# Layer norm rewritten in place, its scalings on ACT, and weight lows made by ACT and an adding DMA

## The chip, the cores and the metric

The kernel runs on one core of a Trainium2 chip. The metric is the device time of one execution in microseconds; smaller is better. TensorE (PE) does the matmuls, VectorE (DVE), ScalarE (ACT) and GpSimd (POOL) the element-wise work, and SyncE (SP) issues nearly all DMAs.

## The reference

A trunk of two layers over 512 tokens of width 1024, float32. Each layer is a half-step feed-forward block, a token mixer (a bidirectional Mamba-2 scan in the first layer, differential attention in the second) and another half-step feed-forward block, each closed by a layer norm:

```python
for i in range(DEPTH):
    ...
    y = swiglu(modulate(x, mods[:, 0]), ffn_w_gate[i, 0], ffn_w_up[i, 0], ffn_w_down[i, 0])
    x = layer_norm(ALPHA * x + 0.5 * gate(0) * y, ln_g[i, 0], ln_b[i, 0])
    u = modulate(x, mods[:, 1])
    ...
    x = layer_norm(ALPHA * x + gate(1) * y, ln_g[i, 1], ln_b[i, 1])
    y = swiglu(modulate(x, mods[:, 2]), ffn_w_gate[i, 1], ffn_w_up[i, 1], ffn_w_down[i, 1])
    x = layer_norm(ALPHA * x + 0.5 * gate(2) * y, ln_g[i, 2], ln_b[i, 2])
```

Here `modulate(x, m) = x * (1 + scale) + shift`, `swiglu(u) = (silu(u @ w_gate) * (u @ w_up)) @ w_down` with an inner width of 2816, and the modulation and gate vectors come from one large projection of a condition vector (adaLN, weights `ada_w`).

## The kernel before, in words

**Layout.** Activations are kept transposed: 8 tiles (`KT`) of 128 channels by 512 tokens. `res[d]` is the residual, `u[d]` the input of the next block. The six blocks are numbered n = 0 to 5: feed-forward 0, Mamba 1, feed-forward 2 and 3, attention 4, feed-forward 5. Layer norm n follows block n.

**Products in two parts.** Matmul operands are split into a high part, rounded to the PE's fp32r format, and a low part, the rest. A product is three matmuls: high by high, high by low, low by high (`mm3`, L158 to L166). For weights, `split` (L102) makes the parts: ACT copies the loaded tile `raw` into `wh` (L119), which rounds it, and DVE subtracts `wh` from `raw` into `wl` (L120). `raw` has 4 buffers in turn, `wh` and `wl` have 3, and 3 more inside a feed-forward block.

**Feed-forward block** (`ffn`, L502). The inner width is worked in three parts of 8, 7 and 7 tiles (`FPARTS`). For each part the kernel first makes the hidden tiles, then does that part's down projection: 8 units, one per output tile d, each with its own weight load (`wdn`), split and 24 or 21 matmuls of 512 columns, and a DVE instruction that adds the result to the residual (`add_res`, L366). "First phase" and "second phase" below are the down projections of the first two parts, `pi` 0 and 1; the third ends in the layer norm. The first hidden tiles of a block are plain (gate and up products, `L535`); from index `first7` on (10 in block 0, otherwise 4) each hidden tile is made with seven products instead of eight, from sums of inputs (`input_forms`, L421, made during the last four plain tiles: DVE L426 to L431, then split by ACT L149 and DVE L150) and sums of weights (`weight_forms`, L442: DVE L459, split by ACT L449 and DVE L450).

**The adaLN stream.** In blocks 0, 2 and 3 the adaLN weights are worked off between other work: `advance(stream, per[1])` puts two of them behind each unit of the first two down projections. Each is one 512 KB load through `raw` and one DVE instruction (L180). Block 5 has none.

**Layer norm** (class `LN`, L260). In the last down projection DVE, ACT and POOL gather the sums as tiles come out (`start`, `feed`); the last units are done in two halves of 256 tokens so that one half's norm runs beside the other half's matmuls. `stats` forms the reciprocal deviation `rb`, spread over the partitions in the PSUM, and centres `res`. `normalize` (L324) then makes the next block's inputs, per tile and half: DVE `t = res * G * rb` (L348), ACT `uh = t + B` (L349), DVE `ul = (t + B) - uh` (L350); ACT copies `rb` into `rs` (L353). `residual` (L355) leaves the scaled residual: two POOL instructions per tile, L359 and L360, 16 per layer norm, needed only by the next block's first `add_res`.

**Order.** Each engine works its own queue in order. The order in the queues is the scheduler's, from the order of the program text and the dependences; a wait at the head of a queue holds all behind it.

Of the kernel before, what the change touches and what calls it, by code (L numbers as in the profile page):

```python
# [46 lines left out]
def hybrid_trunk(tc, xT, cb, par, cst, adaw, wgu, wdn0, wdn1, wdn2, wdt, win, wso, wqk, wv, wao, dist_in, dtp, lam_in, out):  # L47
    nc = tc.nc
    ctx = ExitStack()
    wdn = (wdn0, wdn1, wdn2)  # L50

    cp = ctx.enter_context(tc.tile_pool(name="cp", bufs=1))
    ap = ctx.enter_context(tc.tile_pool(name="ap", bufs=NA))
# [11 lines left out]
    def tmp(name="tmp"):  # L65
        return tp.tile([P, T], F32, tag="t", name=name)
# [24 lines left out]
    def load(src, n=1024):  # L91
        raw = wp.tile([P, 1024], F32, tag="raw", name="raw", bufs=4)
        nc.sync.dma_start(raw[:, :n], src)
        return raw[:, :n]
# [6 lines left out]

    def split(raw, where=None):  # L102

        n = raw.shape[-1]
        if where == "a":
            hi, lo = [], []
            for o in range(0, n, T):
                r = raw[:, o : o + T]
                h, l = big(F32R, "wah"), big(F32R, "wal")
                x = nc.scalar.activation(h, r, AF.Copy)  # L110
                eng = nc.vector if first_split[0] or o else nc.gpsimd
                y = eng.tensor_tensor(out=l, in0=r, in1=h.bitcast(F32), op=ALU.subtract)  # L112
                for a, b in zip((x, y), behind):
                    tc.add_manual_dep(a.ins, b.ins.name, NOSYNC, reason="inputs before weights")
                hi.append(h)
                lo.append(l)
            return [(hi[c // T][:, c % T : c % T + P], lo[c // T][:, c % T : c % T + P]) for c in range(0, n, P)]
        hi, lo = ring()
        nc.scalar.activation(hi[:, :n], raw, AF.Copy)  # L119
        nc.vector.tensor_tensor(out=lo[:, :n], in0=raw, in1=hi[:, :n].bitcast(F32), op=ALU.subtract)  # L120
        return Unit(hi, lo, n)

    def ring():
# [61 lines left out]
    onep, shift, gvec, lnG, lnB, lnag, lnab = {}, {}, {}, {}, {}, {}, {}  # L185
# [74 lines left out]
    class LN:  # L260
# [63 lines left out]
        def normalize(self, a, b, rb):  # L324
            n = self.n
            if n == 5:
                for d in range(KT):
                    t = res[d][:, a:b]
                    nc.vector.scalar_tensor_tensor(
                        out=t, in0=t, scalar=pc(C_LNG + n * 8 + d), in1=rb, op0=ALU.mult, op1=ALU.mult  # L330
                    )
                    nc.scalar.activation(t, t, AF.Identity, bias=pc(C_LNB + n * 8 + d))
                    if d % 2:
                        nc.sync.dma_start(
                            out[(d - 1) * P : (d + 1) * P, a:b].rearrange("(e p) t -> p e t", e=2),
                            resid[:, d - 1 : d + 1, a:b],
                        )
                return
            if self.u is None:
                self.u = [  # L340
                    tuple(ap.tile([P, T], F32R, tag="u", name=x, bufs=2 * KT) for x in ("uh", "ul")) for _ in range(KT)
                ]
                self.rs = ap.tile([P, T], F32, tag="l", name="rs", bufs=3)
            for d in range(KT):
                G, B = lnG[n][:, d : d + 1], lnB[n][:, d : d + 1]
                t = tmp("lt")[:, a:b]
                uh, ul = self.u[d][0][:, a:b], self.u[d][1][:, a:b]
                nc.vector.scalar_tensor_tensor(out=t, in0=res[d][:, a:b], scalar=G, in1=rb, op0=ALU.mult, op1=ALU.mult)  # L348
                nc.scalar.activation(uh, t, AF.Identity, bias=B)  # L349
                nc.vector.scalar_tensor_tensor(  # L350
                    out=ul, in0=t, scalar=B, in1=uh.bitcast(F32), op0=ALU.add, op1=ALU.subtract
                )
            nc.scalar.activation(self.rs[:, a:b], rb, AF.Copy)  # L353

        def residual(self):  # L355
            n = self.n
            if n < 5:
                for d in range(KT):
                    nc.gpsimd.tensor_tensor(out=res[d], in0=res[d], in1=self.rs, op=ALU.mult)  # L359
                    nc.gpsimd.tensor_scalar(  # L360
                        out=res[d], in0=res[d], scalar1=lnag[n][:, d : d + 1],
                        scalar2=lnab[n][:, d : d + 1], op0=ALU.mult, op1=ALU.add,
                    )

    def add_res(d, pd, n, a, b):
        nc.vector.scalar_tensor_tensor(  # L366
# [135 lines left out]
    def ffn(n, stream=None, per=(0, 0), pre=None, first7=FT):  # L502


        forms, making = [], None
        sc = ExitStack()
        extra[0] = sc.enter_context(tc.tile_pool(name=f"wx{n}", bufs=3))
        idx = {0: 0, 2: 1, 3: 2, 5: 3}[n]
        u = next_u[0]
        f = 0  # L510
        pre = pre or first_units(n)
        for pi, nf in enumerate(FPARTS):
            hs = []
            open7 = None
            for _ in range(nf):
                if f >= first7:
                    g = seven(load(wgu[idx, f, 0]), load(wgu[idx, f, 1]), forms, hs)
                    next(g)
                    if open7 is not None:
                        next(open7, None)  # L520
                    next(g)
                    open7 = g
                    f += 1
                    continue
                wg, wu = (pre.pop(0) if pre else split(load(wgu[idx, f, e])) for e in range(2))
                cols = HALVES if f < 3 and n > 0 else FULL
                tag = "mid" if f == 2 else "ln" if f == 3 and n == 0 else "acc"
                pg = acc(tag)
                proj(pg, wg, u, cols=cols)
                pu = acc(tag)  # L530
                proj(pu, wu, u, cols=cols)
                sg = tmp("sg")
                nc.scalar.activation(sg, pg, AF.Silu)
                h = tmp("h")
                nc.vector.tensor_tensor(out=h, in0=sg, in1=pu, op=ALU.mult)  # L535
                hs.append(split_act(h))
                if first7 - 4 <= f < first7:
                    making = making or input_forms(u)
                    forms.append(next(making))
                f += 1  # L540
                if f > 3 or n > 0:
                    advance(stream, per[0])

            if open7 is not None:
                next(open7, None)

            def mk(d):
                return lambda: [(d, split(load(wdn[pi][idx, d], nf * P)))]

            for _ in down_units(n, hs, [mk(d) for d in range(KT)], pi == len(FPARTS) - 1):  # L550
                if pi < 2:
                    advance(stream, per[1])
        extra[0] = None
        sc.close()
# [13 lines left out]
    def ssm(n):  # L568
# [244 lines left out]
        def run(units):  # L813
            for f in units:
                f()
# [6 lines left out]
        dt_chain(pd)  # L822
        run(units_x(0, xs)[2:])
        silu(bc + xs)
        run(units_z(0, zs[0])[:2])
        cur = prepare(0, xs, bc)
        outs, yrs = {}, {}
# [48 lines left out]
    def attention(n):  # L876
# [6 lines left out]
        lt = tmp("lam")  # L883
# [21 lines left out]
        def unit_v(p_):  # L905
            def f():
                w = [split(load(wv[p_, e])) for e in range(2)]
                V[p_] = []
                for b in range(2):
                    pv = acc()  # L910
                    prev = None
                    for t2 in range(2):
                        c = slice((b * 2 + t2) * P, (b * 2 + t2 + 1) * P)
                        terms = []
                        for k in range(KT):
                            wh, wl = w[k // 4].cols((k % 4) * 256, (k % 4 + 1) * 256)
                            terms.append((u[k][0][:, c], u[k][1][:, c], wh, wl))
                        prev = mm3(pv[:, t2 * 256 : (t2 + 1) * 256], terms, prev)
                    V[p_].append(split_act(pv))
            return f  # L920
# [61 lines left out]
        for e in range(2):  # L982
            unit_qk(0, e, HALVES, pre[e])()
        unit_v(0)()
        os_ = {}
        og = []

# [174 lines left out]
```

## Time and profile before

| what | value |
|---|---|
| time, median of 3 runs | 2262.34 us (2256.63 to 2265.38) |
| profiled execution, its own time | 2255.55 us |
| its span, first to last instruction | 2253.7 us |
| PE busy | 2166.1 us (96%) |
| DVE busy | 1817.0 us (81%) |
| ACT busy | 1013.4 us (45%) |
| POOL busy | 407.7 us (18%) |
| DMA moved | 297.02 MB, mean 132 GB/s |

Busy time is the time in which an engine executes; issuing and waiting do not count. A line such as `L120 DVE TENSOR_TENSOR wl<-raw,wh ... x210 | 258.3, 1231 | 81.6` names source line, engine, operation, output and inputs, count, busy time in us, mean of one in ns, and the idle time of the engine just before, with what ended it.

### The profile page before, as it was taken

The numbers are of one execution on the slowest core, as the hardware profiler recorded it, in microseconds if no ns is written. First come the engines' busy times: TensorE is split into PE (matmuls) and PEld (weight loads), VectorE is DVE, ScalarE is ACT, GpSimd is POOL, SyncE is SP. The second block draws the span as 40 slices with busy tenths as digits, with TensorE's granted clock in tenths as the row PEclk, the third lists the DMA queues.
The fourth block names the chain that finished last, engine by engine and source line by source line (L and its number), as shares of the span: only waits on it lengthen the run. The fifth ranks groups of instructions, "written<-read, shape, count | busy, mean of one in ns | idle before, by whom it ended". The sixth has DMA issues, their size and how long they took to land.

```text
span 2253.7 us, 34668 instructions
## 1 busy us (share of the span) xinstructions
PE 2166.1 (96%) x13462; PEld 1886.2 (84%) x13462; DVE 1817.0 (81%) x2982; ACT 1013.4 (45%) x1696; POOL 407.7 (18%) x412
## 2 busy tenths in 40 slices
PE   7999999999999998999999899999999999899998
PEld 5789898866777687999999889899877779889897
DVE  6889898656765689889889998997866679959696
ACT  4324353567656534344453334344555544425353
POOL 3000004344322335000015200003300025000003
PEclk9999999999999989999999999999999999999999
DMA  8873733564544413546442273733211111223231
GB/s 301 273 271 104 242 111 110 123 174 139 168 122 123 134 47 113 196 160 201 146 131 82 79 256 99 244 101 115 67 57 57 57 66 57 103 85 106 92 114 46
DMA packets 88549, 297.02 MB, mean 132 GB/s; under 512 B 9536, under 2 KB 12992, under 8 KB 88384
## 3 DMA queue, kind: packets, MB, share of 16 engines
q1 hardware_dynamic: 88384, 294.81, 40.9%
q8 instruction: 105, 1.72, 0.3%
q14 instruction: 60, 0.49, 0.1%
HBM read 289.53 MB, written 5.24 MB: 131 GB/s over the span
## 4 chain that ended last, share of the span: by engine, by line
PE 55%; DVE 16%; issue 4%; ACT 3%; DMA 2%; POOL 2%; POOLq 0%; ACTq 0%; DVEq 0%; SPq 0%
PE acc L162 44%; PE mid L162 5%; DVE wl L120 2%; PE mid L782 2%; DVE raw L459 2%; DVE lo L150 1%; DVE wl L450 1%; DVE ul L350 1%; DMA raw<-in_wdn 1%; DVE raw L180 1%; PE mid L931 1%; PE ln L162 1%; DVE lt L348 1%; ACT wh L119 1%; PE ln L249 1%
## 5 line engine op out<-in xcount | busy, mean ns | idle before, releaser
L162 PE MATMUL acc<-hi,wh 128*128 128x256 f32 (+1 forms) x1584 | 535.8, 339 | 20.2 <-ACT wh L449 10.0
L162 PE MATMUL acc<-hi,wl 128*128 128x256 f32 (+1 forms) x1584 | 534.9, 338 | 5.6 <-DVE wl L450 5.6
L162 PE MATMUL acc<-lo,wh 128*128 128x256 f32 (+1 forms) x1584 | 533.8, 337 | 1.3 <-DVE lo L150 1.3
L162 PE MATMUL acc<-uh,wh 128*128 128x256 f32 (+1 forms) x1160 | 396.3, 342 | 6.6 <-ACT px L482 6.6
L162 PE MATMUL acc<-ul,wh 128*128 128x256 f32 (+1 forms) x1160 | 393.5, 339 | 0.2 <-DVE ul L1039 0.2
L162 PE MATMUL acc<-uh,wl 128*128 128x256 f32 (+1 forms) x1160 | 391.7, 338 | 1.4 <-DVE wl L120 1.4
L119 ACT ACTIVATE wh<-raw 128x1024 fp32r<-128x1024 f32 (+1 forms) x210 | 213.6, 1023 | 310.7 <-DMA raw<-in_wdn 122.0
L162 PEld LDWEIGHTS acc<-hi,wh 128*128 128x128 f32 x1584 | 304.2, 192 | 58.0 <-ACT wh L449 10.6
L162 PEld LDWEIGHTS acc<-hi,wl 128*128 128x128 f32 x1584 | 304.4, 192 | 36.8 <-DVE wl L450 6.3
L162 PEld LDWEIGHTS acc<-lo,wh 128*128 128x128 f32 x1584 | 304.3, 192 | 33.0 <-DVE lo L150 3.2
L120 DVE TENSOR_TENSOR wl<-raw,wh 128x1024 fp32r<-128x1024 f32 (+1 forms) x210 | 258.3, 1231 | 81.6 <-ACT wh L119 73.4
L449 ACT ACTIVATE wh<-raw 128x1024 fp32r<-128x1024 f32 x198 | 208.7, 1059 | 249.7 <-DVE raw L459 134.3
L450 DVE TENSOR_TENSOR wl<-raw,wh 128x1024 fp32r<-128x1024 f32 x198 | 240.7, 1219 | 33.5 <-ACT wh L449 32.6
L162 PEld LDWEIGHTS acc<-uh,wh 128*128 128x128 f32 x1160 | 222.0, 191 | 39.3 <-issue 9.0
L162 PEld LDWEIGHTS acc<-uh,wl 128*128 128x128 f32 x1160 | 222.1, 192 | 27.8 <-issue 3.9
L162 PEld LDWEIGHTS acc<-ul,wh 128*128 128x128 f32 x1160 | 222.4, 192 | 26.0 <-issue 4.7
L180 DVE SCALAR_TENSOR_TENSOR raw<-raw,cond 128x1024 f32<-128x1024 f32 x144 | 179.3, 1256 | 14.4 <-DMA raw<-in_adaw 13.8
L459 DVE TENSOR_TENSOR raw<-raw 128x512 f32<-128x512 f32 x264 | 183.3, 696 | 5.5
L366 DVE SCALAR_TENSOR_TENSOR resid<-acc,gv,resid 128x512 f32<-128x512 f32 (+1 forms) x172 | 113.0, 659 | 61.1 <-PE acc L162 60.6
L112 POOL TENSOR_TENSOR wal<-raw,wah 128x512 fp32r<-128x512 f32 x13 | 20.9, 1612 | 598.5 <-ACT wah L110 598.4
L277 POOL TENSOR_TENSOR resid<-resid,m 128x512 f32<-128x512 f32 x12 | 20.0, 1687 | 583.5 <-ACT m L274 581.9
L162 PE MATMUL mid<-uh,wh 128*128 128x256 f32 (+2 forms) x380 | 108.6, 286 | 1.4 <-DVE up L491 1.4
(270 smaller groups left out, 4234.8 us busy)
## 6 DMA issues: line engine op xcount, KB each, us to landing
raw<-in_wgu SPq DMA_DIRECT2D x176, 512.0 KB, 4.0
raw<-in_adaw SPq DMA_DIRECT2D x144, 512.0 KB, 4.6
raw<-in_wdn SPq DMA_DIRECT2D x64, 448.0 KB, 3.8
raw<-in_win SPq DMA_DIRECT2D x40, 512.0 KB, 4.4
raw<-in_wdn SPq DMA_DIRECT2D x32, 512.0 KB, 4.4
rw<-scr SPq DMA_DIRECT2D x32, 512.0 KB, 5.5
ch<-scr SPq DMA_DIRECT2D x32, 256.0 KB, 3.7
raw<-in_wso SPq DMA_DIRECT2D x16, 512.0 KB, 3.5
```

The lines of the kernel that those rows point to most:

```text
L119: nc.scalar.activation(hi[:, :n], raw, AF.Copy)
L120: nc.vector.tensor_tensor(out=lo[:, :n], in0=raw, in1=hi[:, :n].bitcast(F32), op=ALU.subtract)
L150: y = nc.vector.tensor_tensor(out=lo, in0=src, in1=hi.bitcast(F32), op=ALU.subtract)
L162: last = nc.tensor.matmul(o, lhsT=a, rhs=b, start=start and j == 0, stop=j == n - 1, skip_group_check=not start)
L180: nc.vector.scalar_tensor_tensor(out=raw, in0=raw, scalar=1.0, in1=cond, op0=ALU.mult, op1=ALU.mult, accum_out=mods[l][:, j : j + 1],)
L249: nc.tensor.matmul(o[:, j * P : (j + 1) * P], lhsT=cols[:, j : j + 1].broadcast_to([P, P]), rhs=ident, start=True, stop=True)
L348: nc.vector.scalar_tensor_tensor(out=t, in0=res[d][:, a:b], scalar=G, in1=rb, op0=ALU.mult, op1=ALU.mult)
L366: nc.vector.scalar_tensor_tensor(out=res[d][:, a:b], in0=pd[:, a:b], scalar=gvec[n][:, d : d + 1], in1=res[d][:, a:b], op0=ALU.mult, op1=A ...
L449: nc.scalar.activation(x[0], r, AF.Copy)
L450: nc.vector.tensor_tensor(out=x[1], in0=r, in1=x[0].bitcast(F32), op=ALU.subtract)
L459: nc.vector.tensor_tensor(out=o, in0=x, in1=y, op=ALU.add)
L782: nc.tensor.matmul(py[hh * 64 : (hh + 1) * 64, cc], lhsT=lhs, rhs=rhs, start=k == 0, stop=k == 2)
```

## The change

It does three things. First, `normalize` multiplies `res` by `rb` in place on DVE (one plain multiplication), and ACT then makes two scaled copies, `uh = G * z + B` in fp32r and `t = G * z + B` in float32; DVE subtracts, `ul = t - uh`. The copy `rs` goes. Second, since `res` now holds the normalized value, the residual is one ACT instruction per tile, `res = lnag * res + lnab`, and POOL has no part in it. These eight instructions are kept in a list `later` and put into the program text behind the next block's first units: two after each of the first four hidden tiles of a feed-forward block, all behind the first SiLUs of the Mamba block, and behind the first value unit of the attention block. Third, in the first two down projections of every feed-forward block the low part of a weight is made without DVE: ACT writes `-raw`, rounded, into `wl`, and a DMA issued by POOL adds `raw` to it in the SBUF. The scratch for DMAs issued this way grows from 1024 to 4096 bytes.

```diff
@@ split @@
         hi, lo = ring()
         nc.scalar.activation(hi[:, :n], raw, AF.Copy)
-        nc.vector.tensor_tensor(out=lo[:, :n], in0=raw, in1=hi[:, :n].bitcast(F32), op=ALU.subtract)
+        if where == "dma":
+            nc.scalar.activation(lo[:, :n], raw, AF.Copy, scale=-1.0)
+            nc.gpsimd.dma_start(lo[:, :n].bitcast(F32), raw, accum_op=ALU.add)
+        else:
+            nc.vector.tensor_tensor(out=lo[:, :n], in0=raw, in1=hi[:, :n].bitcast(F32), op=ALU.subtract)
         return Unit(hi, lo, n)
@@ LN.normalize, LN.residual @@
-                self.rs = ap.tile([P, T], F32, tag="l", name="rs", bufs=3)
             for d in range(KT):
                 G, B = lnG[n][:, d : d + 1], lnB[n][:, d : d + 1]
-                t = tmp("lt")[:, a:b]
+                z, t = res[d][:, a:b], tmp("lt")[:, a:b]
                 uh, ul = self.u[d][0][:, a:b], self.u[d][1][:, a:b]
-                nc.vector.scalar_tensor_tensor(out=t, in0=res[d][:, a:b], scalar=G, in1=rb, op0=ALU.mult, op1=ALU.mult)
-                nc.scalar.activation(uh, t, AF.Identity, bias=B)
-                nc.vector.scalar_tensor_tensor(
-                    out=ul, in0=t, scalar=B, in1=uh.bitcast(F32), op0=ALU.add, op1=ALU.subtract
+                nc.vector.tensor_tensor(out=z, in0=z, in1=rb, op=ALU.mult)
+                for o in (uh, t):
+                    nc.scalar.activation(o, z, AF.Identity, bias=B, scale=G)
+                nc.vector.tensor_tensor(out=ul, in0=t, in1=uh.bitcast(F32), op=ALU.subtract)
+
+        def residual(self):
+            n = self.n
+            def mk(d):
+                return lambda: nc.scalar.activation(
+                    res[d], res[d], AF.Identity, bias=lnab[n][:, d : d + 1], scale=lnag[n][:, d : d + 1]
                 )
-            nc.scalar.activation(self.rs[:, a:b], rb, AF.Copy)
-
-        def residual(self):
-            n = self.n
-            if n < 5:
-                for d in range(KT):
-                    nc.gpsimd.tensor_tensor(out=res[d], in0=res[d], in1=self.rs, op=ALU.mult)
-                    nc.gpsimd.tensor_scalar(
-                        out=res[d], in0=res[d], scalar1=lnag[n][:, d : d + 1],
-                        scalar2=lnab[n][:, d : d + 1], op0=ALU.mult, op1=ALU.add,
-                    )
+            later.extend(mk(d) for d in range(KT) if n < 5)
+
+    later = []
+
+    def scale_residual(k=KT):
+        for f in later[:k]:
+            f()
+        del later[:k]
@@ ffn @@
                 f += 1
+                scale_residual(2 if f < 5 else KT)
                 if f > 3 or n > 0:
                     advance(stream, per[0])
...
-                return lambda: [(d, split(load(wdn[pi][idx, d], nf * P)))]
+                return lambda: [(d, split(load(wdn[pi][idx, d], nf * P), "dma" if pi < 2 else None))]
@@ ssm @@
         silu(bc + xs)
+        scale_residual()
@@ attention @@
         unit_v(0)()
+        scale_residual()
@@ kernel @@
-    nc = bacc.Bacc("TRN2", target_bir_lowering=False, num_devices=1, dynamic_dma_scratch_size=1024)
+    nc = bacc.Bacc("TRN2", target_bir_lowering=False, num_devices=1, dynamic_dma_scratch_size=4096)
```

More of the change, by code (lines that the diff above doesn't have):

```diff
@@ L342, in normalize @@
                 ]
-                self.rs = ap.tile([P, T], F32, tag="l", name="rs", bufs=3)
             for d in range(KT):
                 G, B = lnG[n][:, d : d + 1], lnB[n][:, d : d + 1]
-                t = tmp("lt")[:, a:b]
+                z, t = res[d][:, a:b], tmp("lt")[:, a:b]
                 uh, ul = self.u[d][0][:, a:b], self.u[d][1][:, a:b]
-                nc.vector.scalar_tensor_tensor(out=t, in0=res[d][:, a:b], scalar=G, in1=rb, op0=ALU.mult, op1=ALU.mult)
-                nc.scalar.activation(uh, t, AF.Identity, bias=B)
-                nc.vector.scalar_tensor_tensor(
-                    out=ul, in0=t, scalar=B, in1=uh.bitcast(F32), op0=ALU.add, op1=ALU.subtract
-                )
-            nc.scalar.activation(self.rs[:, a:b], rb, AF.Copy)
+                nc.vector.tensor_tensor(out=z, in0=z, in1=rb, op=ALU.mult)
+                for o in (uh, t):
+                    nc.scalar.activation(o, z, AF.Identity, bias=B, scale=G)
+                nc.vector.tensor_tensor(out=ul, in0=t, in1=uh.bitcast(F32), op=ALU.subtract)
         def residual(self):
             n = self.n
-            if n < 5:
-                for d in range(KT):
-                    nc.gpsimd.tensor_tensor(out=res[d], in0=res[d], in1=self.rs, op=ALU.mult)
-                    nc.gpsimd.tensor_scalar(
-                        out=res[d], in0=res[d], scalar1=lnag[n][:, d : d + 1],
-                        scalar2=lnab[n][:, d : d + 1], op0=ALU.mult, op1=ALU.add,
-                    )
+            def mk(d):
+                return lambda: nc.scalar.activation(
+                    res[d], res[d], AF.Identity, bias=lnab[n][:, d : d + 1], scale=lnag[n][:, d : d + 1]
+                )
+            later.extend(mk(d) for d in range(KT) if n < 5)
[4 more added lines that the diff above has]
+        del later[:k]
     def add_res(d, pd, n, a, b):
```

## The prediction, made before the changed kernel was run

> **What bounds the kernel now.** I read the page first: parts 1 and 2.
>
> ```profile
> span 2253.7 us, 34668 instructions
> PE 2166.1 (96%) x13462; PEld 1886.2 (84%) x13462; DVE 1817.0 (81%) x2982; ACT 1013.4 (45%) x1696; POOL 407.7 (18%) x412
> PE   7999999999999998999999899999999999899998
> DVE  6889898656765689889889998997866679959696
> ```
>
> PE is the bound: 96% busy, so at most 2253.7 - 2166.1 = 87.6 us can be won without touching the matmuls. A change to DVE, ACT, POOL and DMA counts only where PE waits for them. So I looked at stretches where PE is idle while DVE is full. Busy time by stretch gives three, each at the start of a feed-forward block that follows a layer norm (n=1, 2 and 4); the last line is their sum:
>
> ```profile
> 860.00:900.00 40.00, 31.41 (x195) 28.28 (x194) 40.00 (x52) 14.37 (x22) 25.03 (x13) 0.89 0.35 112
> 1255.00:1275.00 20.00, 13.54 (x72) 11.90 (x71) 19.86 (x32) 9.43 (x13) 0.00 (x0) 0.87 0.22 79
> 1915.00:1936.00 21.00, 15.33 (x73) 13.05 (x72) 20.90 (x32) 8.88 (x12) 5.65 (x4) 0.83 0.14 51
> sum 81.00, PE 60.27 PEld 53.23 DVE 80.76 ACT 32.69 POOL 30.68; mean PE 20.09 PEld 17.74 DVE 26.92 ACT 10.90 POOL 10.23
> ```
>
> The columns after the length are PE, PEld, DVE, ACT, POOL, granted clock, DMA share and GB/s. PE is idle for 81.00 - 60.27 = 20.7 us while DVE is busy for 80.76 of 81. The clock column adds a second loss: 0.11 x 40 + 0.13 x 20 + 0.17 x 21 = 10.6 us. Together 31.3 us, the most that these three places can return. Why DVE is late there shows in its instructions by line. The first six rows are one such start, 1226.3 to 1253.8; the next two are whole-run means of clean 512 and 256 wide operations; then come two rows of the page and the two POOL rows of the residual:
>
> ```profile
> L350 DVE SCALAR_TENSOR_TENSOR ul<-lt,lnB,uh 128x256 fp32r<-128x256 f32 x2 | 3.0, 1516 | 0.0
> L150 DVE TENSOR_TENSOR lo<-h,hi 128x512 fp32r<-128x512 f32 x2 | 2.5, 1231 | 0.0
> L426 DVE TENSOR_TENSOR fb<-uh,ul 128x512 f32<-128x512 f32 x2 | 2.5, 1228 | 0.0
> L431 DVE TENSOR_TENSOR fb<-fb 128x256 f32<-128x256 f32 x2 | 2.3, 1167 | 0.0
> L429 DVE TENSOR_TENSOR ft<-ft,fb 128x256 f32<-128x256 f32 x2 | 2.3, 1166 | 0.0
> L180 DVE SCALAR_TENSOR_TENSOR raw<-raw,cond 128x1024 f32<-128x1024 f32 x1 | 2.3, 2303 | 0.0
> L150 DVE TENSOR_TENSOR lo<-sg,hi 128x512 fp32r<-128x512 f32 x66 | 45.3, 687 | 7.0 <-ACT hi L149 7.0
> L490 DVE TENSOR_TENSOR px<-acc,px 128x256 f32<-128x256 f32 x66 | 27.7, 420 | 0.1
> L350 DVE SCALAR_TENSOR_TENSOR ul<-lt,lnB,uh 128x256 fp32r<-128x256 f32 x80 | 45.4, 593 | 0.7 <-ACT uh L349 0.4
> L180 DVE SCALAR_TENSOR_TENSOR raw<-raw,cond 128x1024 f32<-128x1024 f32 x144 | 179.3, 1256 | 14.4 <-DMA raw<-in_adaw 13.8
> L360 POOL TENSOR_SCALAR resid<-resid,lnag,lnab 128x512 f32<-128x512 f32 x40 | 70.5, 1770 | 0.0
> L359 POOL TENSOR_TENSOR resid<-resid,rs 128x512 f32<-128x512 f32 x40 | 62.0, 1570 | 39.0 <-ACT rs L353 39.0
> ```
>
> While POOL scales the residual, DVE operations on two tiles of the SBUF take up to twice their clean time. In this one start that is 2 x (1231 - 687) + 2 x (1228 - 687) + 2 x (1167 - 420) + 2 x (1166 - 420) + (2303 - 1256) + 2 x (1516 - 593) = 8.0 us of DVE time, against the 6.5 us that PE idles there.
>
> **The residual's move.** It takes 80 POOL instructions away, 16 per layer norm, about 8 x (1.77 + 1.57) = 26.7 us each time. With them go the 8.0 us of DVE stretch per start; DVE, not POOL, was on the path. The relief is more than PE's idle in two of the starts and about as much in the first (8.6 us), and a PE that does not stop keeps its clock. I take 28 of the 31.3 us. What would be late next is ACT: the 8 scalings land on it, priced by a 512-wide ACT operation, 8 x 0.63 = 5.0 us per layer norm.
>
> ```profile
> L149 ACT ACTIVATE hi<-sg 128x512 fp32r<-128x512 f32 x66 | 41.5, 629 | 43.9 <-DVE sg L498 43.9
> L348 DVE SCALAR_TENSOR_TENSOR lt<-resid,lnG,ln 128x256 f32<-128x256 f32 x80 | 35.1, 474 | 1.6 <-PE ln L249 1.5
> L349 ACT ACTIVATE uh<-lt,lnB 128x256 fp32r<-128x256 f32 x80 | 36.9, 502 | 35.2 <-DVE lt L348 35.0
> PE acc L162 <- ACT uh L349: 2.2, 3, 1.1
> PE acc L162 <- DVE ul L350: 1.6, 2, 0.8
> ```
>
> ACT is busy 32.7 of 81 us in the three stretches, so its idle time covers the 5.0 us; uncovered, PE could wait behind one pair of scalings, 1.3 us per start. In the Mamba and attention blocks the same 5.0 us follow the first SiLUs and the first value unit: I take zero, with bounds of 5 us lost in either and 3 us won.
>
> **The in-place norm.** Per half tile DVE had 0.474 + 0.593 = 1.07 us; it gets two plain operations like the 0.420 row, 0.84. ACT had 0.502 and gets two, 1.00. So a tile leaves at ACT's 1.00 us instead of DVE's 1.07: nothing. The last two rows (whole run, waits of PE) show all that PE waits for inputs there: 2.2 + 1.6 = 3.8 us, which bounds the gain; the same amount again bounds the loss, if ACT is held up by its squares.
>
> **The lows by ACT and the adding DMA.** For 64 units DVE loses one subtraction (1.1 to 1.2 us), ACT gains one pass (0.95 to 1.06 us), POOL's queue gains one issue. What I had to settle is whether the loads keep up, so I read DMA, DVE, ACT and PE in time order around the two phases of block 2. The first row is block 0's first phase:
>
> ```profile
> 121.00:158.00 37.00, 37.00 (x162) 30.25 (x161) 30.11 (x48) 8.50 (x8) 0.00 (x0) 1.00 0.87 296
> 928.69 0.33 SPq L93 DMA_DIRECT2D raw<-in_wdn  x1
> ...
> 935.32 2.40 SPq L93 DMA_DIRECT2D raw<-in_adaw  x2
> 939.20 0.33 SPq L93 DMA_DIRECT2D raw<-in_wdn  x1
> 932.97 1.06 ACT L119 ACTIVATE wh<-raw 128x1024 fp32r<-128x1024 f32 x1 [0.91 <-DMA raw<-in_wdn]
> 934.07 1.23 DVE L120 TENSOR_TENSOR wl<-raw,wh 128x1024 fp32r<-128x1024 f32 x1 [0.71 <-ACT wh L119]
> 946.39 0.75 DVE L366 SCALAR_TENSOR_TENSOR resid<-acc,gv,resid 128x512 f32<-128x512 f32 x1
> 1043.94 0.95 ACT L119 ACTIVATE wh<-raw 128x896 fp32r<-128x896 f32 x1 [3.56 <-DMA raw<-in_wdn]
> 1060.72 0.50 PE L162 MATMUL acc<-hi,wh 128*128 128x512 f32 x1 [0.99 <-ACT hi L149]
> raw<-in_adaw SPq DMA_DIRECT2D x144, 512.0 KB, 4.6
> raw<-in_wdn SPq DMA_DIRECT2D x32, 512.0 KB, 4.4
> scr<-rows SPq DMA_DIRECT2D x2, 1024.0 KB, 9.2
> out<-resid SPq DMA_DIRECT2D x8, 256.0 KB, 2.2
> ```
>
> PE is full in that window (37.00 of 37.00, 162 matmuls, 0.228 us each), so DVE's relief buys nothing here; ACT, busy 8.50 of 37, has room for its second pass. The larger scratch for POOL's DMA issue costs no time that any row here prices. A unit is 24 matmuls, 5.48 us, in a first phase and 21, 4.80 us, in a second. In blocks 0, 2 and 3 each unit brings three loads (weights, two adaLN rows) through four buffers, in order. So a weight load's buffer is wanted again by the first adaLN load of the next unit, behind which stands the weight load after that. The rows show this: weights at 928.69, buffer free when DVE's subtraction ends (935.3), adaLN issued at 935.32, weights two units on at 939.20. Period: 10.5 / 2 = 5.25 us a unit.
>
> After the change the buffer is held until the adding DMA lands. Call x the time from the end of ACT's second pass to that landing. The period becomes (4.4 load + 2.1 for two ACT passes + x + 1.5 for the issues behind it) / 2; those issues took 3.9 us before (935.32 to 939.20) because adaLN buffers came free late, and a longer period takes that wait away, leaving issues of 0.33 us and their gaps. No row shows x. Below it is bounded by 2.2 us (256 KB out of the SBUF), above by 9.2 us (1024 KB out of the SBUF, as many bytes as the add reads). Nearest is a 512 KB load in these same stretches, 4.6 us; with 0.6 us for POOL's issue, about twice SP's 0.33, I take x = 5.2. Period: 13.2 / 2 = 6.6 us.
>
> That is slower than PE, but the weights are ahead. In block 2's first phase the second unit's ACT pass starts at 932.97 and PE has finished the first unit at 946.4 at the latest; I use 946. After: ready at 932.97 + 2.1 + 5.2 = 940.3, 5.7 us ahead. Over the six units that follow, the supply falls back 6 x (6.6 - 5.48) = 6.7 us: 1.0 us lost. In its second phase: 1043.94 + 1.9 + 5.2 = 1051.0 against 1061, 10.0 ahead; 6 x (6.6 - 4.80) = 10.8: 0.8 us lost. I let these two stand for the three blocks: 3 x 1.8 = 5.4 us. Each phase then hands on no lead, so the next gate and up weights, loaded behind the last unit, come late: an estimate of 1 us each, 6 us. Loss: 11.4 us. Block 5 has no adaLN loads; four weight buffers held for (4.4 + 2.1 + 5.2) give 11.7 / 4 = 2.9 us a unit, under 4.80: nothing. POOL has no other work in these windows (0.00), so nothing queues behind its waiting issue.
>
> **The sum**, on the profiled execution (2255.55 us): 2255.6 - 28 + 11.4 = 2239. That execution is 0.3% under the median shown, 2262.34, so I add half of that difference: 2242. The rivals' times below are on the profiled execution's scale.
>
> **Rivals.** (a) The adding DMA is slower, and the change loses. Adding means reading both tiles. These rows price 256 KB more at 3.5 - 2.5 = 1.0 us, the second read of 512 KB at 2.0 us:
>
> ```profile
> raw<-in_wso SPq DMA_DIRECT2D x16, 512.0 KB, 3.5
> raw<-in_wdt SPq DMA_DIRECT2D x1, 256.0 KB, 2.5
> ```
>
> Then x = 7.2, the period 7.6 us; the leads shrink to 3.7 and 8.0 us and the fall-back grows to 12.7 and 16.8: 9.0 + 8.8 lost per block, 53 in three, 59 with the hand-on: 2255.6 - 28 + 59 = 2287. It decides from x = 5.9 up, where loss and gain are level. For it: the DMA share is 0.87 at 296 GB/s already, so a further transfer lengthens the loads too. Against it: SBUF reads may be quicker than HBM's. The Trainium skill ("Collectives: The Full Stack", The bandwidth ceiling) says an adding transfer issues two source reads per chunk on one ring and so ran at about half a copy's rate; by it this rival holds. No transfer in this trace adds, so the trace cannot confirm it. (b) The add hides wholly: x under 4 us, period under 6.0, no loss: 2255.6 - 31 = 2225. For it: 2.2 us for a small transfer out of the SBUF. (c) Most of the 28 us does not come: the forms wait for ACT (its scalings in front of the splits) where they waited for DVE. With 10 us gained and the 11.4 lost: 2257. Against it: ACT's 60% idle there.
>
> **Chances.** My sum 0.34, (a) 0.31, (b) 0.16, (c) 0.19. A measurement of this kernel tells about 0.5% (11 us) from no change. Of my case 0.28 is faster and 0.06 the same; (b) is faster; (c) is 0.16 same, 0.03 slower; (a) is slower. Faster 0.44, same 0.22, slower 0.34. Range: from (b) with some of the norm's 3.8 us, 2222, to (a) with a little more, 2292; my own case alone 2230 to 2256.
>
> **What would show it.** Residual: no POOL work after the layer norms, the 256-wide DVE operations of the forms near 0.42 us, PE idle gone and its clock at 1.00 after 860, 1255 and 1915. Lows: the time from issue to landing of the POOL-issued DMA with its queue (my x, 5.2 us), SP waiting for that DMA in place of DVE L120, weight loads 6.6 us apart, PE still full in block 2's phases. I am wrong if x passes 5.9 us, if PE's waits for the low tile of the down projection exceed 15 us in all, or if the three starts still idle with ACT named.

## The result: 2.7% slower

| what | before | after |
|---|---|---|
| time, median of the runs side by side | 2261.61 us (2256.63 to 2265.38) | 2322.83 us (2319.84 to 2326.74) |
| ratio, 95% interval | | 1.0273 (1.0247 to 1.0299) |
| profiled execution | 2255.55 us | 2324.32 us |

61 us were lost where 20 us of gain were predicted; the time lies outside the predicted range (2222 to 2292). Of the eight executions of e4_raw5 below one was in the chip's slow state (2965.76 us at a granted clock of 0.654), so its time is the median of the other seven, 2272.21 us; with the eighth it is 2273.55, from which the 49 and the 60 us in two later expectations come. The page of the changed kernel, its first lines, the slices of PE and DVE, and its DMA queues:

```profile
span 2322.5 us, 34945 instructions
PE 2186.1 (94%) x13462; PEld 1898.5 (82%) x13462; DVE 1704.3 (73%) x2918; ACT 1135.3 (49%) x1870; POOL 329.5 (14%) x396
PE   7989989999999989988999998889999998999998
DVE  6859598656766689677688958678776678948496
q1 hardware_dynamic: 88384, 294.81, 39.6%
q0 software_dynamic: 9216, 31.46, 7.4%
```

DVE was relieved as meant (1817.0 to 1704.3 us). But PE, the bound, now stands still for 2322.5 - 2186.1 = 136 us instead of 88, and its busy time rose by 20 us for the same 13462 matmuls, at a lower granted clock behind the pauses (rows below).

**Where the time went.** I cut both spans at the first and the last matmul of each down projection phase (PE `acc<-hi,wl`, 128x512) and subtracted. Between these profiled executions the difference is 68.8 us (7.6 more than between the medians).

| stretch | after - before, us |
|---|---|
| from the last down projection ahead to the first one of blocks 2, 3 and 5 (the mixers, the layer norms, the three starts) | -24.3 |
| the first phases of blocks 0, 2 and 3 | +30.9 |
| the second phases of these blocks | +3.1 |
| the six stretches of hidden tiles behind these phases | +54.5 |
| block 5 behind its start | +4.6 |

The start gain came, most of it. The starts, by stretches of the changed kernel that cover the input forms (columns as in the prediction), and three of the forms' rows in the second of them:

```profile
890.00:930.00 40.00, 39.18 (x280) 36.55 (x278) 40.00 (x67) 24.37 (x36) 0.00 (x0) 1.00 0.38 119
1285.00:1319.00 34.00, 34.00 (x240) 31.84 (x240) 32.03 (x58) 19.34 (x29) 0.00 (x0) 1.00 0.25 81
1970.00:2003.00 33.00, 33.00 (x235) 30.97 (x234) 32.57 (x56) 21.50 (x33) 0.00 (x0) 1.00 0.21 69
```

```profile
L436 DVE TENSOR_TENSOR fb<-uh,ul 128x512 f32<-128x512 f32 x4 | 2.7, 684 | 0.0
...
L441 DVE TENSOR_TENSOR fb<-fb 128x256 f32<-128x256 f32 x4 | 1.7, 420 | 0.0
...
L439 DVE TENSOR_TENSOR ft<-ft,fb 128x256 f32<-128x256 f32 x4 | 1.7, 418 | 0.0
```

POOL is gone, the operations that took 1228 and 1167 ns take 684 and 420, and PE idles 0.8 us of 107 at full clock.

The loss is not mainly inside the phases whose weights were changed. More than half of it lies in the hidden tiles behind them. These stretches by windows, first two of before (of block 2, then the sum of all six), then the same of the changed kernel:

```profile
982.60:1051.80 69.20, 69.20 (x578) 68.88 (x578) 64.08 (x102) 32.99 (x51) 0.00 (x0) 1.00 0.40 129
1093.60:1162.80 69.20, 69.20 (x578) 68.89 (x578) 60.80 (x93) 34.43 (x53) 0.00 (x0) 1.00 0.35 108
...
sum 424.90, PE 421.12 PEld 414.32 DVE 381.92 ACT 204.17 POOL 0.00; mean PE 70.19 PEld 69.05 DVE 63.65 ACT 34.03 POOL 0.00
```

```profile
1017.40:1094.80 77.40, 71.05 (x580) 70.10 (x579) 66.55 (x108) 37.80 (x56) 2.61 (x3) 0.96 0.49 142
1136.00:1213.80 77.80, 73.29 (x578) 72.38 (x577) 70.17 (x105) 38.77 (x57) 0.00 (x0) 0.93 0.36 110
...
sum 479.30, PE 437.94 PEld 427.23 DVE 418.54 ACT 231.02 POOL 7.77; mean PE 72.99 PEld 71.21 DVE 69.76 ACT 38.50 POOL 1.29
```

The same 578 matmuls filled 69.20 us without a gap before. Now PE idles 479.3 - 437.9 = 41.4 us in the six (3.8 before), and needs 16.8 us more for the same matmuls at a clock of 0.93 to 0.96. What it waits for, from the changed kernel's waits of PE, and of ACT; then ACT's timeline from 1084 to 1096:

```profile
PE acc L167 <- DMA wl<-raw: 18.9, 8, 5.6
PE acc L167 <- ACT sg L498: 18.0, 6, 5.5
...
PE acc L167 <- ACT hi L154: 11.5, 8, 2.9
PE acc L167 <- ACT px L492: 9.9, 5, 3.7
```

```profile
ACT wh L120 <- DMA raw<-in_wdn: 184.2, 46, 10.2
```

```profile
1089.07 0.95 ACT L120 ACTIVATE wh<-raw 128x896 fp32r<-128x896 f32 x1 [8.14 <-DMA raw<-in_wdn]
1089.93 0.40 ACT L507 ACTIVATE sg<-px 128x256 f32<-128x256 f32 x1
1090.23 0.93 ACT L122 ACTIVATE wl<-raw 128x896 fp32r<-128x896 f32 x1
1091.09 0.63 ACT L154 ACTIVATE hi<-sg 128x512 fp32r<-128x512 f32 x1
1091.62 0.36 ACT L498 ACTIVATE sg<-acc 128x256 f32<-128x256 f32 x1
```

Only 18.9 us are a wait for a low. The other rows are hidden-tile work on ACT (SiLU, copies and splits). The timeline shows why it is late at the end of such a stretch: the pass of a late weight, the third of the next phase, stands at the head of ACT's queue, 8.14 us without its data, and the SiLUs behind it wait too. PE, which waits for `sg`, idles 5.5 us there (from 1086.5). Before, that weight's pass stood behind the SiLU in the queue, and waited 0.21 us:

```profile
1047.87 0.42 ACT L497 ACTIVATE sg<-px 128x256 f32<-128x256 f32 x1 [2.70 <-DVE px L496]
1048.50 0.95 ACT L119 ACTIVATE wh<-raw 128x896 fp32r<-128x896 f32 x1 [0.21 <-DMA raw<-in_wdn]
```

So it is not only the load that came later: in blocks 2 and 3 the scheduler also put the pass ahead of the SiLU. DVE's queue added to it. The instruction that makes this SiLU's input (`px`, L506) ended at 1087.4, behind an adaLN instruction that had waited 1.97 us for its load; over the whole run DVE waited 136.8 us for adaLN loads, 13.8 before. In the six stretches together PE waits 16 us for `sg`, nearly all at their ends, and 25 us for other work, most of it near their starts, where the gate and up weights come late.

The adding DMA itself, by POOL's group and the medians from issue to landing:

```profile
L123 POOL DMA_DIRECT2D wl<-raw x64 | 55.6, 869 | 891.5 <-ACT wl L122 525.4
...
raw<-in_wdn SPq DMA_DIRECT2D x32, 512.0 KB, 5.1
wl<-raw POOLq DMA_DIRECT2D x32, 512.0 KB, 7.0
...
wl<-raw POOLq DMA_DIRECT2D x32, 448.0 KB, 6.4
```

With the 0.3 us that POOL starts behind ACT, x is 7.3 us for a full unit and 6.7 for a short one, 7.0 on average. The queue q0 took 0.074 x 2322.5 x 16 = 2750 us of engine time for 64 transfers, 43 us each or 2.7 us of all 16 engines; the loads of q1 come to 1.6 us of all 16 per 512 KB.

### The profile page after: what moved, and what is told of

It is laid out like the page before. It is cut to its first block, busy times and chain, and to the rows that moved or that the text cites. A ratio compares the mean times of both kernels' runs of the same rounds, so it can differ in the third digit from the quotient of the medians.

```text
span 2322.5 us, 34945 instructions
## 1 busy us (share of the span) xinstructions
PE 2186.1 (94%) x13462; PEld 1898.5 (82%) x13462; DVE 1704.3 (73%) x2918; ACT 1135.3 (49%) x1870; POOL 329.5 (14%) x396
## 5 line engine op out<-in xcount | busy, mean ns | idle before, releaser
L167 PE MATMUL acc<-hi,wl 128*128 128x256 f32 (+1 forms) x1584 | 540.9, 342 | 24.3 <-DMA wl<-raw 18.9
L185 DVE SCALAR_TENSOR_TENSOR raw<-raw,cond 128x1024 f32<-128x1024 f32 x144 | 177.8, 1238 | 145.8 <-DMA raw<-in_adaw 136.8
L167 PEld LDWEIGHTS acc<-uh,wl 128*128 128x128 f32 x1160 | 221.8, 191 | 26.7 <-issue 3.9
L125 DVE TENSOR_TENSOR wl<-raw,wh 128x1024 fp32r<-128x1024 f32 (+1 forms) x146 | 178.7, 1224 | 51.1 <-ACT wh L120 42.7
L123 POOL DMA_DIRECT2D wl<-raw x64 | 55.6, 869 | 891.5 <-ACT wl L122 525.4
L376 DVE SCALAR_TENSOR_TENSOR resid<-acc,gv,resid 128x512 f32<-128x512 f32 (+1 forms) x172 | 112.9, 658 | 41.4 <-PE acc L167 41.0
L167 PE MATMUL mid<-uh,wl 128*128 128x256 f32 (+2 forms) x380 | 107.5, 283 | 0.0
```

What stands on the lines that cost most here:

```text
L123: nc.gpsimd.dma_start(lo[:, :n].bitcast(F32), raw, accum_op=ALU.add)
L167: last = nc.tensor.matmul(o, lhsT=a, rhs=b, start=start and j == 0, stop=j == n - 1, skip_group_check=not start)
L185: nc.vector.scalar_tensor_tensor(out=raw, in0=raw, scalar=1.0, in1=cond, op0=ALU.mult, op1=ALU.mult, accum_out=mods[l][:, j : j + 1],)
L376: nc.vector.scalar_tensor_tensor(out=res[d][:, a:b], in0=pd[:, a:b], scalar=gvec[n][:, d : d + 1], in1=res[d][:, a:b], op0=ALU.mult, op1=A ...
```

## The experiments

Twelve runs, each timed beside the kernel before on the same chip. The columns behind the ratio are microseconds against before in the profiled executions, cut as above (to about 0.2 us): the starts with the mixers ahead, the six phases, the six stretches of hidden tiles behind them. Below, "the norm part" is the in-place norm with the residual on ACT.

| kernel | us | ratio to before (95%) | starts | phases | hidden |
|---|---|---|---|---|---|
| changed kernel | 2322.83 | 1.0273 (1.0247 to 1.0299) | -24.3 | +34.0 | +54.5 |
| e1_norm: norm part alone | 2226.48 | 0.9853 (0.9837 to 0.9870) | -31.6 | +1.0 | +2.1 |
| e2_lows: lows alone | 2353.12 | 1.0416 (1.0393 to 1.0439) | +11.4 | +33.2 | +51.6 |
| e3_block5: lows in block 5 only | 2230.81 | 0.9873 (0.9853 to 0.9893) | -33.8 | +2.9 | +2.9 |
| e8_pool: residual by one POOL instruction | 2225.96 | 0.9851 (0.9836 to 0.9866) | -30.0 | +1.0 | +1.0 |
| e9_pooltwo: by two POOL instructions | 2254.18 | 0.9977 (0.9967 to 0.9986) | -4.6 | -0.2 | +1.5 |
| e10_noscale: before, no residual scaling | 2224.78 | 0.9849 (0.9834 to 0.9863) | -34.6 | +1.2 | +0.6 |
| e5_copy: copying DMA in place of the adding | 2270.12 | 1.0063 (1.0035 to 1.0092) | -33.5 | +14.3 | +33.2 |
| e4_raw5: changed, five load buffers | 2272.21 | 1.0056 (1.0036 to 1.0077) | -37.0 | +16.9 | +27.8 |
| e7_traffic: norm part + adding traffic | 2269.70 | 1.0049 (1.0033 to 1.0066) | -32.8 | +17.3 | +26.7 |
| e13_hold: norm part + buffer held | 2266.87 | 1.0031 (1.0017 to 1.0046) | -34.6 | +24.0 | +25.0 |
| e11_raw3: norm part, three load buffers | 2286.43 | 1.0115 (1.0092 to 1.0137) | -24.3 | +9.1 | +41.3 |
| e12_raw5: norm part, five load buffers | 2213.28 | 0.9797 (0.9783 to 0.9812) | -36.0 | -5.1 | -7.2 |

**The two parts.** First the norm part alone, then the lows alone:

```diff
-                return lambda: [(d, split(load(wdn[pi][idx, d], nf * P), "dma" if pi < 2 else None))]
+                return lambda: [(d, split(load(wdn[pi][idx, d], nf * P), None))]
```

> The changed kernel with its lows made by DVE again in every phase; the norm in place and the residual on ACT stay. Theory (the loss lies in the lows, the stretch of DVE beside POOL's residual was real): 28 us under before, about 2234, the three starts (feed-forward 2, 3, 5) without PE idle and with a full clock. Rival (the residual on ACT itself delays the blocks): within 10 us of before, 2252 to 2272.

> The kernel before with only the lows of the first two down projections made by ACT and the adding DMA (scratch 4096). Theory that the two parts add: the changed kernel is 61 us slower, the norm part wins 28, so this is 89 us slower than before, about 2351. Rival, that they depend on each other (PE reaches the phases earlier when the starts are shorter, so the weights' lead is spent there): under 75 us slower, below 2337.

They came to -34 us and +93 us; together 59, against the measured 61. So the parts add, the norm part beats both kernels, and the loss belongs to the lows alone. (e2_lows is the kernel before with only the other branch of `split` and the larger scratch, which e1_norm has too, without a loss.)

**Block 5**, where there is no adaLN stream:

```diff
+                ... "dma" if pi < 2 and n == 5 else None ...
```

> The changed kernel with the adding DMA in block 5 alone, where no adaLN loads run. Both theories of the loss (the DMA engines are full; the buffers are held) need those loads: within 5 us of the run with the norm alone. Rival (the add's own latency of about 7 us or ACT's second pass costs PE): 15 us or more slower than it, a quarter of the loss of 70 or more.

2230.81, 4 us above the norm part, with intervals that overlap. In the profiled executions, which lie 8.2 us apart, block 5's first phase is 5.8 us longer and the hidden tiles behind it 1.5 us. The same DMA costs little where the load stream is thin.

**Is POOL the cause of the idle starts?** The gain could also come from cheaper DVE instructions in the norm. First the norm part with the residual by one POOL instruction per tile:

```diff
-            later.extend(mk(d) for d in range(KT) if n < 5)
+            for d in range(KT if n < 5 else 0):
+                nc.gpsimd.tensor_scalar(
+                    out=res[d], in0=res[d], scalar1=lnag[n][:, d : d + 1],
+                    scalar2=lnab[n][:, d : d + 1], op0=ALU.mult, op1=ALU.add,
                 )
```

> As the run with the norm alone, but POOL scales the residual, one TENSOR_SCALAR per tile at the old place instead of two instructions (about 14 of 26.7 us of POOL per layer norm). Theory (DVE is stretched while POOL works): half of the gain is lost, 2244 to 2252, the stretched DVE operations are there for half as long. Rival (the gain comes from DVE's cheaper instructions in the norm): the same time as the run with the norm alone, within 5 us.

The whole gain stayed, though POOL still worked 62.8 us:

```profile
L362 POOL TENSOR_SCALAR resid<-resid,lnag,lnab 128x512 f32<-128x512 f32 x40 | 62.8, 1586 | 18.8 <-ACT lt L354 18.8
```

By that alone the prediction's cause could have been wrong, for POOL still worked beside DVE: at block 3's start from 1216.6 to 1230.3, and the forms began at 1227.1. (The next expectation calls POOL done before the forms start; this trace shows 3.2 us of overlap.) So two more kernels: the norm part with two POOL instructions per tile again (first times a tile of ones), and the kernel before with the residual's scaling left out, a part that it then does not compute.

> The in-place norm as in the change, the lows by DVE, and the residual back on POOL with two instructions per tile (times a tile of ones, then scale and bias), so that POOL works about as long as before, 26 us per layer norm. Theory 'POOL beside DVE': with POOL's long work back beside the forms, the gain of 34 us shrinks to 5 to 10 us, near 2250 to 2256, and the starts of blocks 2, 3 and 5 go back up by 6 to 10 us each. Theory 'cheaper norm on DVE' (the gain comes from tensor_tensor in place of scalar_tensor_tensor): it stays near 2227. One POOL instruction per tile kept the whole gain, with POOL done before the forms start; if two keep it too, POOL is not the cause.

> The kernel before with the residual's scaling left out (that part isn't computed), norm and lows as before. Theory 'POOL beside DVE': the gain of the starts comes with this alone, 28 us or more off, near 2230. Theory 'cheaper norm on DVE': near before, 2255 to 2260. If both contribute, between, 2235 to 2250.

With two instructions 28 of the 34 us were back (2254.18). Without any residual work, and with the old norm, the gain was whole (2224.78; -35.5 against -34.0, intervals overlapping). POOL's work on the residual is the cause; the norm's instructions are at most a small part (e9_pooltwo, which has the new ones, is 5 us under before). The starts of e9_pooltwo by windows, then some rows of DVE and POOL in one of them, in order of time:

```profile
866.00:902.00 36.00, 31.89 (x213) 29.11 (x211) 35.93 (x55) 15.49 (x24) 10.62 (x7) 0.96 0.29 97
1237.00:1275.00 38.00, 34.72 (x230) 31.98 (x230) 37.90 (x60) 14.65 (x23) 13.71 (x8) 0.96 0.22 71
1898.00:1935.00 37.00, 33.27 (x222) 31.03 (x221) 36.83 (x54) 15.05 (x24) 13.74 (x8) 0.94 0.21 71
```

```profile
1242.90 1.87 POOL L366 TENSOR_SCALAR resid<-resid,lnag,lnab 128x512 f32<-128x512 f32 x1
1243.08 1.21 DVE L463 TENSOR_TENSOR wl<-raw,wh 128x1024 fp32r<-128x1024 f32 x1
...
1244.74 1.45 POOL L365 TENSOR_TENSOR resid<-resid,onez 128x512 f32<-128x512 f32 x1
...
1244.96 1.77 DVE L158 TENSOR_TENSOR lo<-ft,hi 128x512 fp32r<-128x512 f32 x1
1246.66 0.41 DVE L444 TENSOR_TENSOR fb<-fb 128x256 f32<-128x256 f32 x1
```

DVE's subtraction of 1244.96, 0.68 us when clean, began 0.22 us after POOL's multiplication of two tiles and ended 0.54 us after that one's end (1246.19): it did most of its work behind it. Beside POOL's other instruction, the scale and bias of one tile, the subtraction of 1243.08 took 1.21 us, its clean time. It is so over the whole run. In e9_pooltwo 58 DVE operations on two SBUF tiles overlapped the multiplication and took 75.8 us together, 39.2 when clean; 44 met only the scale and bias and took 31.0 us, 30.4 when clean; in e8_pool 73 met it and took 56.0 us, 48.7 when clean. So the stretch comes nearly all from the instruction on two tiles, and this, more than an earlier end, is why one instruction per tile cost nothing. No run has two instructions on one tile each to test it alone.

The Trainium skill ("SBUF — State Buffer", SBUF: two separate sides) says that DVE operations with two SBUF inputs and GpSimd share ports under an exclusive lock, held for a whole instruction. The rows beside the multiplication agree; those beside the scale and bias, which reads the SBUF too, do not (1.21 us begun 0.18 us after it).

**Two reads?** The add replaced by a copy (the low part is then the whole weight):

```diff
-            nc.gpsimd.dma_start(lo[:, :n].bitcast(F32), raw, accum_op=ALU.add)
+            nc.gpsimd.dma_start(lo[:, :n].bitcast(F32), raw)
```

> The changed kernel with a plain copying DMA in place of the adding one: same issue, same 512 KB written, but the low part is then the whole weight, not the rest. If the add pays for two reads: engine time per DMA falls from 43 to about 26 us (that of a load of the same size), landing from issue from 7.0 to about 5.3 us, the time to about 2280. If the cost is POOL's issue and the queue, not the second read: landing stays above 6.3 us and the time above 2305.

```profile
q0 software_dynamic: 7168, 31.46, 3.6%
...
wl<-raw POOLq DMA_DIRECT2D x32, 512.0 KB, 5.5
...
wl<-raw POOLq DMA_DIRECT2D x32, 448.0 KB, 5.1
```

The copy takes half the engine time (3.6 against 7.4%) and lands 1.5 us sooner; the Trainium skill's rule of two source reads ("Collectives: The Full Stack", The bandwidth ceiling), which the prediction cites, agrees. But a copy with x near 5.6 still costs 2270.12 - 2226.48 = 44 us more than the norm part. So the second read, with the longer landing that comes with it, is about half of the loss; the copying transfer alone is enough for the rest.

**Traffic or buffers?** The transfer does two things: it loads the DMA engines, and it holds the load buffer about 7 us longer. The changed kernel with five buffers (`bufs=5` for `raw`); the norm part plus two adding DMAs per unit of the first two phases, each half a unit, from `wh` into tiles that nothing reads (traffic without holding `raw`); the norm part with three buffers; with five:

```diff
+            for k in range(2):
+                nc.gpsimd.dma_start(dum[k][:, : n // 2], hi[:, k * n // 2 : (k + 1) * n // 2].bitcast(F32), accum_op=ALU.add)
```

> The changed kernel with five buffers for loaded weights instead of four. Held-buffer theory (a weight's buffer is held 14 us, two weights share two of four buffers, so a unit takes 14.3 / 2 = 7.1 us): with one more buffer the period falls to about 5.7 us and most of the 70 us in the six phases goes: 2250 to 2270. Full-engines theory (loads and adds together keep the 16 DMA engines 0.93 busy): the period stays at 6.8 to 7.1 us, 2310 to 2325.

> The run with the norm alone (lows by DVE, so the loaded weight's buffer is free early), and beside it, per unit of the first two phases, two adding DMAs of half the size from the high part into tiles that nobody reads: the same bytes moved, no buffer of the loads held, nobody waiting. Full-engines theory: a loss like the changed kernel's, 2290 to 2325. Held-buffer theory: within 10 us of the run with the norm alone, about 2235 to 2245.

> In-place norm and residual on ACT, lows by DVE, and three load buffers in place of four: a buffer is missing, as in the change the adding DMA holds one for 7 us longer, but no byte more is moved. Theory 'buffer held': the six streamed phases lose some 50 us together, near 2275. Theory 'traffic alone': within 10 us of 2227.

> In-place norm and residual on ACT, lows by DVE, and five load buffers in place of four. In the change the fifth buffer returned 49 us; here the weights are ahead of PE already in the streamed phases, so both theories expect little: 2215 to 2228, the rest being the phases' own waits for loads.

A fifth buffer returned 51 us of the loss, and traffic without holding `raw` cost 43. Neither theory came out whole. With five buffers the time is near the held-buffer theory's, but the weight loads of the phases stayed 6.9 us apart, as the other theory had it. And 2269.70 lies between the two ranges; the traffic is not quite pure either, since ACT waited 26.2 us for `wh` buffers that these DMAs were still reading. The loads themselves became slower in e7_traffic (medians to landing; before 4.6 and 4.4 us):

```profile
q0 software_dynamic: 18432, 31.47, 8.0%
...
raw<-in_adaw SPq DMA_DIRECT2D x144, 512.0 KB, 5.7
...
raw<-in_wdn SPq DMA_DIRECT2D x32, 512.0 KB, 6.4
dum<-wh POOLq DMA_DIRECT2D x64, 256.0 KB, 6.8
```

A missing buffer, without a byte more, cost 60 us, 39 of them in the hidden tiles; but it is missing everywhere, so it does not size the hold in the phases. And of the 51 us that the fifth buffer returned, it gives 13 without any adding DMA. To size the hold alone took one more kernel: the norm part and, per unit of the first two phases, two adding DMAs of 8 KB, one waiting for the other, out of `raw`.

```diff
+            for k in range(2):
+                nc.gpsimd.dma_start(dum[trn[0] % 2], raw[:8, k * 256 : k * 256 + 256], accum_op=ALU.add)
```

> In-place norm and residual on ACT, lows by DVE, four load buffers; per unit of the first two down projections two adding DMAs of 8 KB each, one behind the other, out of the load buffer into a tile that nothing reads. They hold the buffer some 7 us longer, as the changed kernel's adding DMA does, but move 1.6% of its bytes, and the low is ready as early as before. Theory 'buffer held': the weight loads come some 7 us apart again and the six streamed phases lose 40 to 50 us together, near 2270. Theory 'traffic alone': no loss, near 2227. By the difference of the runs with four and five buffers (96 against 60 us), the hold is worth 36 us, so 2263.

2266.87: the hold alone costs 40 us. SP's waits for it are as long as those for the adding DMA (the queue, then e13_hold's row, then the changed kernel's):

```profile
q0 software_dynamic: 4096, 1.06, 0.5%
```

```profile
SPq L98 <- DMA dum<-raw: 206.8, 51, 8.9
```

```profile
SPq L93 <- DMA wl<-raw: 207.4, 63, 8.6
```

From the second weight load of a phase to the last, weight loads were issued on average every 5.27 us before, 6.14 with the traffic alone, 6.71 with the hold alone and 7.22 in the changed kernel. By these two runs 43 + 40 = 83 of the 96 us between the norm part and the changed kernel; the remaining 13 were not isolated: the low that is ready later than by DVE and block 5's 5 us are in neither kernel, and in both the SiLU kept its place ahead of the third weight's pass. e12_raw5, the norm part with five buffers, is the fastest: 2213.28, 2.0% under before. Of its 13 us over the norm part most lie in the hidden tiles and phases.

## Why the prediction was wrong, point by point

- **The residual's move, 28 us: right in size and cause.** In the norm part alone the stretches with the three starts gave 31.6 us; cut once more at the last matmul of the mixers' output projections, 2.9 of it lie in the mixers with the norms ahead of them (Mamba 0.3, attention 2.6; they were put at zero, with 3 us won as a bound), so 28.8 are the starts' own. In the changed kernel 21.2 of these were left. e9_pooltwo and e10_noscale show the cause. Two readings were coarse: some DVE operations took up to 2.8 times their clean time (1167 against 420 ns), not twice, and by e9_pooltwo nearly all of the stretch comes from one of POOL's two instructions. ACT's scalings were hidden, as taken (e1_norm and e8_pool differ by 0.5 us).
- **The in-place norm at nothing: nearly.** With the long POOL work kept it was worth 5 us (e9_pooltwo, 0.9977, interval 3 to 7 us), near the 3.8 that bounded it; e10_noscale has the old norm and is 1.7 us faster than e1_norm, but leaves the residual's scaling out altogether.
- **x = 5.2: too small, 7.0 measured.** The row chosen as nearest, a plain load of 4.6 us, prices one read. Rival (a), priced by a second read of 2.0 us, had 7.2.
- **The period, 6.6 us: right for the second phases by luck, too short for the first.** From second to last load the spacing was 6.7 us in the second phases (448 KB a unit) and 7.7 in the first (512 KB), where x was longer and the loads landed after 5.1 us, not the 4.4 of the sum. With x = 6.7 in the second phases the prediction's sum would have been over 7 us, so that its 6.6 met the measured 6.7 is luck. Rival (a) had 7.6. The base of 5.25 was right (5.27 over all six).
- **The lead held, the loss did not follow.** In block 2's first phase the second unit's low landed at 963.5 and PE ended the first unit near 968.9: 5.4 us, 5.7 predicted. But the last low landed at 1010.5, so the period was 47.0 / 6 = 7.8 and by the prediction's own formula 6 x (7.8 - 5.48) - 5.4 = 8.5 us were lost, not 1.0. Windows of that phase, before and after, show PE idle for 0.3 and 8.1 us, 6.2 of these waiting for the low:

```profile
936.70:982.60 45.90, 45.65 (x205) 37.14 (x204) 40.83 (x65) 13.27 (x15) 0.00 (x0) 1.00 0.78 263
```

```profile
959.70:1017.40 57.70, 49.62 (x205) 39.21 (x204) 30.11 (x53) 17.03 (x19) 5.22 (x6) 0.94 0.89 261
```

  The other 4.0 us of this phase's 11.8 are the clock, 0.94, which the sum left out. Over the three blocks the first phases lost 30.9 us (predicted 3.0). The second ones lost 3.1 (predicted 2.4), which is luck in part: block by block it is 3.3, -0.6 and 0.3, and PE reached them late, after the pauses ahead.
- **The hand-on, "an estimate of 1 us each, 6 us": the step that failed most, 54.5 us in its place.** The prediction asked what stands behind the waiting instruction on POOL and SP, but not on ACT. There the first pass waited 184 us for its weights (122 before), and in blocks 2 and 3 a hidden tile's SiLU, ahead of that pass before, now stood behind it. Then gate and up weights came late, and the clock fell behind the pauses. Of the 41 us that PE idled in these stretches 16 lie at their ends (SiLU) and 25 elsewhere, most near their starts; 16.8 us more are longer matmuls at the lower clock. This split is read from the waits and timelines; no run isolates its parts.
- **The break-even x = 5.9: wrong.** The copy, x about 5.6, costs more (44 us) than the norm part gains (34). For the same reason rival (a), right in mechanism and in x, gave 2287 and not 2323: it priced 59 us where 96 were lost, its hand-on being the same 6 us. Its first phases came near (27 us, 30.9 measured), its second ones not (26 us, 3.1 measured).
- **Block 5 at nothing: nearly.** 4 us by e3_block5, not clear of noise; 4.6 in the changed kernel's profile.
- **The signs named** came: no POOL work after the norms, forms at 0.42 us, SP waiting for `wl<-raw`, x over 5.9, and 18.9 us of waits for the low, over the 15 given as the mark of being wrong. "PE still full in block 2's phases" did not.

## What to carry to other kernels

Price a transfer inside the SBUF by the time for which it holds its source buffer and by its engine time, not by whether its result is ready: here each of the two, nearly alone, ate more than the whole gain of 34 us. When a load gets later, look at the in-order queue of the engine that receives it, since what stands behind the wait there may feed another stage; here more of the loss lay behind the phases than in them. See also whether the scheduler has changed the order in that queue. And before moving work off GpSimd, see which of its instructions stretches DVE: here the multiplication of two tiles did, and with the scale and bias of one tile alone the time was as good as with none.

## What the runs showed of the hardware

- An adding DMA inside the SBUF took 43 us of engine time for a unit (480 KB on average) and landed after 7.0 us for 512 KB, a copy of the same bytes 20 us and 5.5; POOL's issue took 0.87 us, where 0.6 had been estimated.
- Transfers between other tiles slow the loads: with 8.0% of the engines' span added (e7_traffic), the 512 KB loads of down-projection weights went from 4.6 us (norm part) to 6.4.
- DVE operations on two SBUF tiles took 75.8 us, 39.2 when clean, beside POOL's multiplication of two tiles, and 31.0 us, 30.4 when clean, beside its scale and bias of one tile alone (e9_pooltwo).
- Pauses went with a lower clock. In the 24 us after the changed kernel's phase that ended at 1136, PE idled 4.5 us and its granted clock was 0.79:

```profile
1136.00:1160.00 24.00, 19.49 (x130) 18.76 (x129) 21.38 (x30) 10.75 (x14) 0.00 (x0) 0.79 0.30 89
```
